# Encoder with mixture of experts on one Trainium2 core: the stage from output projection to first expert in hand order, first pair's tokens by one-hot products

## The chip, the cores and the metric

The kernel runs on one core of one Trainium2 chip. The metric is the device time of one execution in microseconds (us), the median of several runs. Three runs of the kernel before gave 1571.79, 1573.48 and 1576.59 us.

## The reference

Two layers on 512 tokens of width 1024, fp32. In each, a mixer makes a 512x1024 concatenation of heads, which is multiplied with `w_out`; then comes a LayerNorm, then a mixture of 32 experts in 4 groups of 8 (best group, best two experts in it), then a LayerNorm again. What the change touches is this piece, once per layer:

```
x = layer_norm(ALPHA * x + concat @ w_out, ln1_g, ln1_b)          # 512 x 1024
grp, exp = x @ w_grp + b_grp, x @ w_exp + b_exp                   # 4 and 32 logits of a token
g = argmax(grp); top2 = top_k(exp[g], 2)                          # two experts of a token
for e in experts:
    h = silu(x[tokens of e] @ w_gate[e]) * (x[tokens of e] @ w_up[e])
    ffn[tokens of e] += gate * (h @ w_down[e])
x = layer_norm(ALPHA * x + ffn, ln2_g, ln2_b)
```

The weights of the experts are 6.3 MB each, some 200 MB per layer, and are read once.

## The kernel before, in words

Tokens stand in four tiles of 128. Weights come through 16 slots of 1 MB that are shared (`slot`, `free`) and, in the expert stage, 7 or 8 more; `pump` issues the next load on SP's queue as soon as a slot is free, so the expert weights of a layer begin to arrive during the output projection, until all slots are full. A further load is issued only when the first expert has given slots back.

**The stage in question, `out_rest`** (from L452), is written as a string of steps (`PLAN`, L37), one for each layer, that are issued in that order; TensorE's and VectorE's final order is the scheduler's, except where `<` in front of a step says that it is to come after the last marked instruction. The steps: `b` and `o` are the output projection of one tile (each of two halves of the heads: 24 matmuls of 512 columns); `n` is a tile's residual sum (L506) and LayerNorm (`layer_norm`, L545), after which the tile is written to DRAM (`x1d`, L509); `t` turns a tile by eight transposes and two ScalarE copies (`moe_turn`); `l` makes its 36 logits by eight matmuls and adds the bias (`moe_logits`, L977, L981); `r` chooses the two experts and builds the one-hot slots (`moe_route`, L983); `H` and `R` give slots back; `S` is below. Tiles 1 and 2 are routed together, by instructions of twice the width. LayerNorm has a short form, two VectorE instructions (L558, L559) around GpSimd's power (L555, L556), and a long one on ScalarE, VectorE and GpSimd; the plan says which tile has which.

`moe_route` finds a maximum, marks where it stands, weighs the marks to keep the first, and does this for group, best and second expert. The marks of the two experts go to `rab` (L1028, bf16). TensorE counts by products with a triangle and with ones how many tokens before this one chose the same expert; with that `rpos` (L1035) holds a token's place and `S` (L1037) is, for four experts, a one-hot matrix of tokens by 64 places.

Step `S` (`start`) multiplies `S` with the token numbers (`moe_tokens`, `idr`), gets the row numbers `ridx` (L1095) and fetches the tokens of the pairs of experts 0 and 1 from `x1d` by an indirect DMA (`moe_fetch`, L1121). In `moe`, `moe_fit` (L1048) checks that no expert has more than 64 tokens; every engine loads that flag (`rover`) into a register and branches (L1283, L1284) past a general path, which is not taken with these inputs. Then `moe_gates` makes the gates, `features(0)` turns the fetched tokens by eight transposes into PSUM and a ScalarE copy (L1130), and the first expert's matmuls (`up`, 64x512 outputs) start. A pair of experts shares a 128-token tile.

Of the kernel before, what the change touches and what calls it, by code (L numbers as in the profile page):

```python
# [11 lines left out]
F32 = mybir.dt.float32  # L12
# [8 lines left out]
P = 128  # L21
D = 1024
# [14 lines left out]
PLAN = (("w w b2 b3 o0 H o2 n0 o1 o3 n2 R t0 n1 n3 <l0 <t3 <t1 <l1 <t2 l2 r0 <l3 r12 r3 S",  # L37
         (1, 3), (0, 2)),
        ("o0 o1 o3 o2 n1 R n0 <n3 n2 t3 <t1 <t0 <l1 t2 <l2 <l3 <l0 <r0 r12 r3 S",
         (1, 2, 3), ()))  # L40
# [41 lines left out]
class Kernel:  # L82
# [159 lines left out]
    def setup(self):  # L242
# [12 lines left out]
        wt = self.wt = c.tile([P, 8], F32, name="wt")  # L255
        for i in range(8):
            nc.gpsimd.memset(wt[:, i:i + 1], 0.5 ** i)
# [194 lines left out]
    def out_rest(self, pool, gbuf, m, plan, opt):  # L452


        res = [self.residual(m, t) for t in range(NT)]

        def begin(t):
            self.out_open(t)
            for q in self.order[:2]:
                self.out_mm(t, (2 * q, 2 * q + 1), q == self.order[0], False)  # L460

        def half_room():

            for q in self.order[:2]:
                self.free(*self.out_w[q])
            self.free(*self.catbuf.pop(self.order[0] // 2))

        def out(t):
            if t not in self.out_ps:
                begin(t)  # L470
            for q in self.order[2:]:
                if q not in self.out_w:
                    self.out_w[q] = self.next_w()
                self.out_mm(t, (2 * q, 2 * q + 1), False, q == self.order[-1])

        def turn(t):
            if t < 2:
                ps[t] = [self.pb()]
                halves = [ps[t][0][:, 0:512], ps[t][0][:, 512:D]]
                z = pool.tile([P, D], F32, name="mxT", bufs=2)  # L480
            else:
                halves = ps[t] = [self.pa(), self.pa()]
                z = rows[0][:, (t % 2) * D:(t % 2 + 1) * D]
            xT[t] = z.rearrange("p (j n) -> p j n", j=KJ)
            self.moe_turn(m, xT[t], res[t], halves)

        def logits(t):
            return self.moe_logits(m, xT[t], t, ps[t][0][:, 0:36])

        def route(*ts):  # L490

            z = ps[ts[-1]]
            last, f = self.moe_route(m, pool, ts, z[0][:, 512:D] if len(z) == 1 else z[1])
            for t in ts:
                self.rel(*ps[t])
            late.append(f)
            return last

        ps, xT, late = {}, {}, []

        def norm(t):
            tiles, halves = self.out_ps.pop(t)
            w = D // len(tiles)
            for i, z in enumerate(tiles):
                x = res[t][:, i * w:(i + 1) * w]
                self.nc.vector.scalar_tensor_tensor(x, x, ALPHA, z, op0=OP.mult, op1=OP.add)  # L506
            self.rel(*tiles)
            last = self.layer_norm(pool, res[t], gbuf, t in opt[0], t in opt[1])
            self.nc.scalar.dma_start(self.x1d[t * P:(t + 1) * P, :], res[t])  # L509
            return last  # L510

        def room():

            self.spare += 4
            if len(self.catbuf) == 2:
                half_room()
            for q in self.order[2:]:
                self.free(*self.out_w[q])
            self.free(*self.catbuf.popitem()[1])
            rows.append(self.slot())  # L520
            m.update(xbuf=self.slot(), xr=self.slot(), sc=self.slot(F32R))
            m["S"] = m["sc"][:, 0:D].rearrange("p (t e n) -> p t e n", t=NT, n=CAP)
            self.nc.gpsimd.memset(m["xr"], 0.0)
            self.spare -= 4

        def start():

            self.free(rows.pop())
            for p in range(2):
                ps = self.pa()  # L530
                self.moe_tokens(m, m["S"][:, :, 2 * p:2 * p + 2], self.idr, ps, p)
                self.rel(ps)
                self.moe_fetch(m, p, False)

        rows = []
        steps = dict(b=begin, H=half_room, w=self.prep_w, o=out, n=norm, t=turn, l=logits, r=route, R=room, S=start)
        last = None
        for step in plan.split():
            with self.tc.issue_after(last.ins) if step[0] == "<" else nullcontext():
                step = step.lstrip("<")  # L540
                last = steps[step[0]](*(int(t) for t in step[1:])) or last
        for f in late:
            f()

    def layer_norm(self, pool, x, gbuf, short, pool_beta):  # L545

        nc = self.nc
        gb = gbuf.rearrange("p (k n) -> p k n", k=2)
        st = pool.tile([P, 4], F32, name="lnas", bufs=4)
        mean, var, rs, nmr = (st[:, i:i + 1] for i in range(4))  # L550
# [4 lines left out]
        nc.gpsimd.tensor_scalar(rs, var, 1.0, LN_EPS, op0=OP.mult, op1=OP.add)  # L555
        nc.gpsimd.tensor_tensor(rs, rs, self.mhalf[:, 0:1], op=OP.pow)  # L556
        if short:
# [1348 lines left out]
```

## Time and profile before

| | |
|---|---|
| median of three runs | 1573.48 us |
| the profiled execution, by the same clock | 1578.68 us |
| its span in the trace | 1576.7 us |
| PE busy | 1493.6 us (95%) |
| DVE, ACT, POOL busy | 679.7, 444.0, 200.6 us |
| mean granted TensorE clock | 0.973 of full |
| read from HBM | 463 MB |

All times in the trace are us from the start of the span. PE is TensorE's matmul stream, PEld its weight loads, PEq its sequencer, DVE VectorE, ACT ScalarE, POOL GpSimd, SPq SyncE's DMA queue. A row of the timeline has start, duration, engine, line, operation, output<-inputs, sizes and how many instructions it merges, and in brackets the engine's idle time before it with what ended it. A plain fp32 matmul stands in the trace as two records, a transpose or an fp32r matmul as one: the eight logit matmuls of a tile are 16 records.

### The profile page before, as it was taken

What the parts mean: (1) busy time and instruction counts of PE and PEld (TensorE: products, weight loads), DVE (VectorE), ACT (ScalarE), POOL (GpSimd) and SP (SyncE); (2) the same over time, 40 slices, a digit from 0 to 9 for tenths busy, and PEclk for the clock granted to TensorE, in tenths of its full rate; (3) what the DMA queues carried; (4) which work ended last, traced back from release to release, by engine and by line L of the source; (5) the groups of instructions that cost most, each with busy time, mean ns of one, the idle gap of its engine ahead of it and who ended that gap; (6) DMA issues with size and microseconds to landing.
All of it is one profiled execution on the core that took longest, in us unless ns stands there. A gap on an engine that the chain in (4) does not pass through costs nothing. (4 is left out here: it accounts for less than half of the span.)

```text
span 1576.7 us, 19665 instructions
## 1 busy us (share of the span) xinstructions
PE 1493.6 (95%) x7801; PEld 897.0 (57%) x7801; DVE 679.7 (43%) x1198; ACT 444.0 (28%) x771; POOL 200.6 (13%) x296
## 2 busy tenths in 40 slices
PE   7999999879999999999999899996999999999997
PEld 6888888755444444444358687675444444444433
DVE  4555655443334334343445634364333433434334
ACT  4545522022121121111236534512212112111222
POOL 2322211321000000010022200031100000001001
PEclk9999999959999999999999999996999999999998
DMA  7311133759999999999963111276999999999993
GB/s 238 108 54 54 54 112 129 306 166 386 425 425 426 426 426 426 425 427 425 427 236 107 54 54 54 80 306 269 391 426 426 426 427 426 426 425 426 426 426 134
DMA packets 107131, 465.62 MB, mean 295 GB/s; under 512 B 13152, under 2 KB 48448, under 8 KB 57744
## 3 DMA queue, kind: packets, MB, share of 16 engines
q1 hardware_dynamic: 98848, 444.86, 69.5%
q0 software_dynamic: 6448, 13.06, 2.3%
q10 hardware_dynamic: 1728, 6.29, 1.1%
q8 instruction: 65, 1.06, 0.3%
q14 instruction: 42, 0.34, 0.1%
HBM read 463.16 MB, written 9.44 MB: 300 GB/s over the span
## 5 line engine op out<-in xcount | busy, mean ns | idle before, releaser
L217 PE MATMUL pa<-big 128*64 128x512 f32 (+3 forms) x4168 | 834.5, 460 | 10.3 <-ACT big L207 3.0
L217 PEld LDWEIGHTS pa<-big 128*128 128x128 f32 (+1 forms) x4168 | 451.6, 166 | 320.8 <-issue 273.9
L217 PE MATMUL pa<-big,hs 128*64 128x512 f32 x992 | 224.8, 592 | 0.0
L1187 DVE SCALAR_TENSOR_TENSOR big<-pa,rgate,big 64x512 fp32r<-64x512 f32 x120 | 90.0, 750 | 213.4 <-ACT big L1186 213.3
L1142 DVE SCALAR_TENSOR_TENSOR big<-big,pb 128x1024 f32<-128x1024 f32 x112 | 134.3, 1220 | 70.7 <-PE pb L217 68.8
L217 PEld LDWEIGHTS pa<-big,hs 128*64 128x64 f32 x992 | 72.9, 137 | 140.7 <-issue 136.2
L217 PE MATMUL pb<-big 128*128 128x512 f32 (+1 forms) x512 | 141.8, 414 | 5.2 <-DVE big L1142 4.2
L1186 ACT ACTIVATE big<-pa,rgate 64x512 fp32r<-64x512 f32 x120 | 81.9, 683 | 218.9 <-PE pa L217 170.2
L1157 DVE TENSOR_TENSOR h<-pa,h 64x512 f32<-64x512 f32 x64 | 44.4, 694 | 226.7 <-ACT h L1156 226.7
L217 PEld LDWEIGHTS pb<-big 128*128 128x128 f32 x512 | 91.3, 188 | 44.2 <-issue 20.2
L1156 ACT ACTIVATE h<-pa 64x512 f32<-64x512 f32 x64 | 37.7, 589 | 268.2 <-PE pa L217 268.2
L207 DVE TENSOR_TENSOR big<-big 128x2048 fp32r<-128x2048 f32 (+2 forms) x38 | 77.3, 2033 | 66.2 <-ACT big L207 47.4
L207 ACT CAST big<-big 128x2048 fp32r<-128x2048 f32 (+2 forms) x39 | 64.7, 1664 | 57.6 <-PE pa L217 22.5
L1121 POOL DMA_INDIRECT big<-x1d,ridx x32 | 34.0, 1062 | 356.1 <-DVE ridx L1095 269.2
L1120 POOL MEMSET big<- 128x1024 f32 x28 | 26.7, 955 | 315.8 <-PE pb L222 315.7
L1130 ACT COPY big<-pb 128x1024 f32<-128x1024 f32 x32 | 32.4, 1012 | 120.8 <-PE pb L222 120.8
L222 PE MATMUL pb<-eye,big 128*128 128x128 f32 x304 | 46.4, 298 | 20.0 <-DVE y L1082 6.2
L222 PEld LDWEIGHTS pa<-eye,h 64*128 64x128 f32 x256 | 35.5, 209 | 37.9 <-DVE big L1187 24.3
L217 PE MATMUL pb<-big,C 128*128 128x512 f32 x192 | 53.9, 412 | 2.5 <-DVE big L1142 2.5
L222 PEld LDWEIGHTS pb<-eye,big 128*128 128x128 f32 x304 | 40.7, 196 | 25.5 <-issue 20.1
L1167 DVE COPY hs<-pa 128x256 f32<-128x256 f32 x64 | 27.0, 422 | 43.6 <-PE pa L222 43.5
L217 PEld LDWEIGHTS pb<-big,C 128*128 128x128 f32 x192 | 33.3, 188 | 19.4 <-issue 9.7
(326 smaller groups left out, 1228.2 us busy)
## 6 DMA issues: line engine op xcount, KB each, us to landing
big<-in_moe_w_gate_dram SPq DMA_DIRECT2D x128, 1024.0 KB, 19.5
big<-in_moe_w_up_dram SPq DMA_DIRECT2D x128, 1024.0 KB, 19.6
big<-in_moe_w_down_dram SPq DMA_DIRECT2D x128, 1024.0 KB, 19.6
big<-in_ev_w_in_dram SPq DMA_DIRECT2D x24, 512.0 KB, 5.6
big<-in_od_w_in_dram SPq DMA_DIRECT2D x7, 1024.0 KB, 5.6
big<-in_x_dram SPq DMA_DIRECT2D x8, 512.0 KB, 4.2
big<-in_ev_w_out_dram SPq DMA_DIRECT2D x4, 1024.0 KB, 4.7
x1d<-big ACTq DMA_DIRECT2D x8, 512.0 KB, 7.8
```

What stands on the lines that cost most here:

```text
L207: ins = self.nc.scalar.copy(hi, src), (sub or self.nc.vector).tensor_tensor(lo, src, hi.bitcast(F32), op=OP.subtract)
L217: return self.nc.tensor.matmul(o, a, b, start=start, stop=stop, skip_group_check=True)
L222: self.nc.tensor.transpose(o, a, self.eye[s, s])
L1120: self.nc.gpsimd.memset(x, 0.0)
L1121: self.nc.gpsimd.indirect_dma_start(x, None, self.x1d[:, :], bass.IndirectOffsetOnAxis(m["idx"][:, pair:pair + 1], 0), bounds_check=T - 1, ...
L1130: self.nc.scalar.copy(xn, ps.rearrange("p (j n) -> p j n", j=KJ))
L1142: self.nc.vector.scalar_tensor_tensor(x, x, ALPHA if first else 1.0, ps, op0=OP.mult, op1=OP.add)
L1156: self.nc.scalar.activation(h, o[0:64], AF.Silu)
L1157: self.nc.vector.tensor_tensor(h, o[64:128], h, op=OP.mult)
L1167: self.nc.vector.tensor_copy(hs.rearrange("p j n -> p (j n)"), ps[:, 0:4 * CAP])
L1186: last = self.nc.scalar.activation(hi, src, AF.Copy, scale=g[a:a + 64])
L1187: self.nc.vector.scalar_tensor_tensor(yl[a:a + 64, s], src, g[a:a + 64], hi.bitcast(F32), op0=OP.mult, op1=OP.subtract)
```

## The change

- The two plan strings go. The steps of both layers stand as one list of calls inside a manual schedule that fixes the order on TensorE and VectorE. Tile by tile: the last output projections carry the turn and the logits of tiles 0 and 1 between them, and the choice of a tile's experts runs on VectorE between the norms.
- All tiles have the short LayerNorm, split into `ln_stats` and `ln_apply`; adding epsilon moves from GpSimd to VectorE.
- The choice (`moe_choose`) works on all 32 expert logits, with the other groups pushed down by -3e38, always on one tile, 13 instructions of VectorE. It writes `A0` and `A1`, which were made later before.
- The tokens of pair 0 are no longer fetched: `gather(t)` multiplies a tile's normalised tokens with its one-hot slots, eight fp32 matmuls of 128x128 per tile, summed over tiles in PSUM and copied by two ScalarE copies into `xbuf`. So `features(0)` and its fetch go. Pair 1 is fetched as before.
- Half of the projection's slots are given back before tile 0's projection in both layers (only in layer 0 before), and the working slot `rows` is not needed.
- `moe_fit` moves ahead of the last gather.

```diff
@@ out_rest @@
+        def half_room():
+            self.spare += 3
...
+            m.update(xbuf=self.slot(), xr=self.slot(), sc=self.slot(F32R))
...
+        def gather(t):
+            if t == 0:
+                m["g"] = self.pb()
+            xv = res[t].rearrange("p (k j) -> p j k", j=KJ)
+            S = m["S"][:, t, 0:2].bitcast(F32).rearrange("p e n -> p (e n)")
+            for j in range(KJ):
+                self.mm(m["g"][:, j * P:(j + 1) * P], xv[:, j, :], S, t == 0 and j % 4 == 0, t == NT - 1)
...
-        for step in plan.split():
-            with self.tc.issue_after(last.ins) if step[0] == "<" else nullcontext():
-                step = step.lstrip("<")
-                last = steps[step[0]](*(int(t) for t in step[1:])) or last
+        with self.tc.manual_schedule(engines={mybir.EngineType.PE, mybir.EngineType.DVE}):
+            begin(2)
+            begin(3)
+            half_room()
+            out(0)
+            norm(0, total(0))
+            out(1)
+            norm(1, total(1))
+            out(2)
+            turn(0)
+            norm(2, total(2))
+            out(3, last[0])
+            logits(0)
+            choose(0)
+            turn(1)
+            out(3, last[1])
+            room()
+            st = total(3)
+            logits(1)
+            count(0)
+            place(0)
+            norm(3, st)
+            turn(2)
+            choose(1)
+            logits(2)
+            count(1)
+            place(1)
+            gather(0)
+            choose(2)
+            turn(3)
+            gather(1)
+            count(2)
+            place(2)
+            logits(3)
+            gather(2)
+            choose(3)
+            count(3)
+            pc = self.moe_fit(m)
+            place(3)
+            gather(3)
+            self.moe_fits(m, pc)
+            for t in range(NT):
+                self.moe_slots(m, t, 1)
+            z = self.pa()
+            self.moe_tokens(m, m["S"][:, :, 2:4], self.idr, z, 1)
+            self.rel(z)
+            self.moe_fetch(m, 1, False)
+            for a in range(2):
+                s = slice(a * 512, (a + 1) * 512)
+                nc.scalar.copy(m["xbuf"][:, s], m["g"][:, s])
@@ ln_stats, ln_apply (layer_norm before) @@
-        nc.gpsimd.tensor_scalar(rs, var, 1.0, LN_EPS, op0=OP.mult, op1=OP.add)
-        nc.gpsimd.tensor_tensor(rs, rs, self.mhalf[:, 0:1], op=OP.pow)
+        nc.vector.tensor_scalar(st[:, 2:3], st[:, 1:2], LN_EPS, None, op0=OP.add)
+        nc.gpsimd.tensor_tensor(st[:, 2:3], st[:, 2:3], self.mhalf[:, 0:1], op=OP.pow)
...
+        self.nc.vector.scalar_tensor_tensor(x, x, st[:, 0:1], gb[:, 0], op0=OP.subtract, op1=OP.mult)
+        self.nc.vector.scalar_tensor_tensor(x, x, st[:, 2:3], gb[:, 1], op0=OP.mult, op1=OP.add)
@@ moe_choose (moe_route before) @@
+        def first_hot(o, v, mx, k, op):
+            fm = r.tile([P, 1], F32, name="fm", bufs=8)
             nc.vector.tensor_reduce(mx, v, axis=AX.X, op=OP.max)
+            nc.vector.scalar_tensor_tensor(o, v, mx, wt[:, 0:k], op0=OP.is_equal, op1=OP.mult, accum_out=fm)
+            nc.vector.tensor_scalar(o, o, 2.0, fm, op0=OP.mult, op1=op)
...
+        first_hot(A0, s, m["m12"][:, 0, t:t + 1], NE, OP.is_gt)
+        nc.vector.scalar_tensor_tensor(s, A0, -3.0e38, s, op0=OP.mult, op1=OP.add)
+        first_hot(A1, s, m["m12"][:, 1, t:t + 1], NE, OP.is_gt)
+        nc.vector.tensor_tensor(m["ab"][:, t, :], A0, A1, op=OP.add)
@@ moe @@
-        self.moe_fit(m)
...
-            features(0)
             up(0, 0)
```

TensorE in layer 0, from the last output projections to the first counts; before:

```order
L217 MATMUL pa<-big 128x512 x30
L217 MATMUL pb<-big 128x512 x24
L217 MATMUL pa<-big 128x512 x24
L217 MATMUL pb<-big 128x512 x24
L217 MATMUL pa<-big 128x512 x24
L222 MATMUL pb<-eye,big 128x128 x8
L222 MATMUL pa<-eye,big 128x128 x8
L222 MATMUL pb<-eye,big 128x128 x8
L217 MATMUL pa<-y_106,big 128x36 x4
L217 MATMUL pb<-y_106,mxT 128x36 x16
```

The same place in the change (its matmuls are issued at L213, its transposes at L218):

```order
L213 MATMUL pb<-big 128x512 x48
L213 MATMUL pa<-big 128x512 x24
L218 MATMUL pb<-eye,big 128x128 x8
L213 MATMUL pa<-big 128x512 x12
L213 MATMUL pb<-y_106,mxT 128x36 x8
L218 MATMUL pb<-eye,big 128x128 x8
L213 MATMUL pa<-big 128x512 x12
L213 MATMUL pb<-y_106,mxT 128x36 x8
L213 LDWEIGHTS tri
L213 MATMUL pb<-rab,tri 128x32
L218 MATMUL pa<-eye,big 128x128 x8
```

The turns (`eye`) and logits (128x36) of tiles 0 and 1 have moved in among the projections of tile 3, and the rest of the tiles follow one by one; the projections of 512 columns are as many as before.

VectorE in layer 0, from the last tile's sum (L506) to the first choice; before:

```order
L506 SCALAR_TENSOR_TENSOR big<-big,pa 128x512 x2
L553 BN_STATS lnst<-big 128x6 x2
L554 BN_AGGR lnas<-lnst 128x2
L558 SCALAR_TENSOR_TENSOR big<-big,lnas 128x1024
L559 SCALAR_TENSOR_TENSOR big<-big,lnas 128x1024
L981 TENSOR_TENSOR y_106<-pb,y_106 128x36 x2
```

In the change, from the end of tile 0's choice (`rab`) over the last tile's sum (L490) to the start of tile 1's choice:

```order
L1042 TENSOR_TENSOR rab<-y_106 128x32
L490 SCALAR_TENSOR_TENSOR big<-big,pa 128x512 x2
L592 BN_STATS lnst<-big 128x6 x2
L593 BN_AGGR lnas<-lnst 128x2
L594 TENSOR_SCALAR lnas<-lnas 128x1
L1053 SCALAR_TENSOR_TENSOR rpos<-pb,rab 128x32
L1057 TENSOR_TENSOR big<-io,rpos 128x128
L600 SCALAR_TENSOR_TENSOR big<-big,lnas 128x1024
L601 SCALAR_TENSOR_TENSOR big<-big,lnas 128x1024
L1021 TENSOR_TENSOR y_106<-pb,y_106 128x36
```

Tile 3's sum and norm now stand behind the choice of tile 0, and the choice of tile 1 behind that norm.

TensorE in layer 0, end of the stage; before:

```order
L217 LDWEIGHTS tri
L217 MATMUL pa<-rab,tri 128x32
L217 LDWEIGHTS ones
L217 MATMUL pa<-rab,ones 128x32
L217 MATMUL pa<-idr,big 128x2 x2
L1283 TENSOR_LOAD rover
L1284 COMPARE_AND_BRANCH
```

and in the change:

```order
L213 LDWEIGHTS ones
L213 MATMUL pa<-rab,ones 128x32
L213 MATMUL pb<-big 128x128 x8
L213 MATMUL pa<-idr,big 128x2 x4
L1300 TENSOR_LOAD rover
L1301 COMPARE_AND_BRANCH
```

The last gather (`pb<-big 128x128 x8`) has come in between the counts and the load of the flag; behind the branch, the eight transposes of the fetched tokens are gone, so that the first expert follows.

## Rows read from the trace of the kernel before

**Rows 1.** The page, part 2: what the DMA engines moved in 40 equal slices.
```profile
GB/s 238 108 54 54 54 112 129 306 166 386 425 425 426 426 426 426 425 427 425 427 236 107 54 54 54 80 306 269 391 426 426 426 427 426 426 425 426 426 426 134
```

**Rows 2.** Timeline of PE at the end of either expert stage.
```profile
787.03 3.65 PE L217 MATMUL pa<-big 128*64 128x512 f32 x14 [1.43 <-DMA big<-in_moe_w_up_dram]
...
1534.16 3.65 PE L217 MATMUL pa<-big 128*64 128x512 f32 x14 [1.35 <-DMA big<-in_moe_w_up_dram]
```

**Rows 3.** Windows of 1 us on PE, layer 0: busy (instructions), granted clock, DMA share, GB/s.
```profile
317.00:318.00 1.00, 1.00 (x7) 0.50 1.07 287
...
320.00:321.00 1.00, 1.00 (x11) 1.00 0.98 397
...
324.00:325.00 1.00, 1.00 (x7) 0.50 1.06 446
...
330.00:331.00 1.00, 1.00 (x7) 0.50 0.00 0
...
354.00:355.00 1.00, 1.00 (x8) 1.00 0.00 0
```

**Rows 4.** Timeline of PE, layer 0, output projection to first expert.
```profile
290.02 5.60 PE L217 MATMUL pb<-big 128*128 128x512 f32 x24
...
306.34 5.61 PE L217 MATMUL pa<-big 128*128 128x512 f32 x24
...
317.47 1.91 PE L222 MATMUL pb<-eye,big 128*128 128x128 f32 x8
...
344.43 1.94 PE L222 MATMUL pb<-eye,big 128*128 128x128 f32 x8 [6.24 <-DVE y L1082]
347.47 13.53 PE L217 MATMUL pa<-big 128*64 128x512 f32 x48 [1.10 <-ACT big L1130]
```

**Rows 5.** Timeline of PE, layer 1, the same stage.
```profile
1045.80 16.48 PE L217 MATMUL pa<-big 128*128 128x512 f32 x72
...
1096.30 12.88 PE L217 MATMUL pa<-big 128*64 128x512 f32 x48 [1.54 <-ACT big L1130]
```

**Rows 6.** Matmuls of 16 or 32 records: 36 and 128 columns; eight transposes (PE).
```profile
1067.74 1.95 PE L217 MATMUL pb<-y,mxT 128*128 128x36 f32 x16
...
327.93 3.63 PE L217 MATMUL pa<-y,big 128*128 128x36 f32 x16
...
1109.10 1.15 PE L222 MATMUL pb<-eye,big 128*128 128x128 f32 x8
...
273.32 3.74 PE L217 MATMUL pa<-rvg,pt 128*128 128x128 f32 x32
```

**Rows 7.** Timeline of DVE, layer 0: a short norm, tile 3's last choice, its slots.
```profile
308.88 1.22 DVE L506 SCALAR_TENSOR_TENSOR big<-big,pb 128x1024 f32<-128x1024 f32 x1
...
313.70 1.28 DVE L559 SCALAR_TENSOR_TENSOR big<-big,lnas 128x1024 f32<-128x1024 f32 x1 [0.72 <-POOL lnas L556]
...
335.42 0.16 DVE L998 TENSOR_REDUCE y<-sel 128x1 f32<-128x8 f32 x1
...
336.16 0.17 DVE L1026 TENSOR_TENSOR o<-o,o 128x8 f32<-128x8 f32 x1
...
337.12 0.42 DVE L1037 TENSOR_TENSOR big<-io,rpos 128x256 fp32r<-128x256 f32 x1
```

**Rows 8.** Timeline of POOL, layer 0: epsilon of the norm in rows 7.
```profile
311.75 1.28 POOL L555 TENSOR_SCALAR lnas<-lnas 128x1 f32<-128x1 f32 x1 [0.38 <-DVE lnas L554]
```

**Rows 9.** Timeline of DVE, layer 1: tile 3's slots, the last to be made.
```profile
1087.37 0.43 DVE L1037 TENSOR_TENSOR big<-io,rpos 128x256 fp32r<-128x256 f32 x1
```

**Rows 10.** PE's sequencer at the branch (both layers), and at an earlier flag's load.
```profile
L1284 PEldq COMPARE_BRANCH  x2: 3326/4546/5765, 338.2 to 1088.3; - x2
...
L1619 PEldq TENSOR_LOAD <-steep x1: 314/314/314, 1012.5 to 1012.5; - x1
...
1014.30 3.89 PE L217 MATMUL pb<-big 128*128 128x512 f32 x14
```

**Rows 11.** The chain that ended last: up matmuls of later experts.
```profile
1142.75 10.45 PE pa L217 x48
```

More of the change, by code (lines that the diff above doesn't have):

```diff
@@ L254, in setup @@
         nc.vector.memset(self.ones, 1.0)
-        wt = self.wt = c.tile([P, 8], F32, name="wt")
-        for i in range(8):
-            nc.gpsimd.memset(wt[:, i:i + 1], 0.5 ** i)
+        wt = self.wt = c.tile([P, NG, EPG], F32, name="wt")
+        for i in range(EPG):
+            nc.gpsimd.memset(wt[:, :, i], 0.5 ** i)
         tid = self.tid = c.tile([P, NT], F32, name="tid")
@@ L490, in route @@
[L490 to L537, printed above, removed]
-        for step in plan.split():
-            with self.tc.issue_after(last.ins) if step[0] == "<" else nullcontext():
-                step = step.lstrip("<")
-                last = steps[step[0]](*(int(t) for t in step[1:])) or last
@@ L542, in out_rest, with choose, count, place @@
-        for f in late:
-            f()
-    def layer_norm(self, pool, x, gbuf, short, pool_beta):
+            z = ps[t]
+            self.moe_logits(m, xT[t], z[0][:, 0:36])
+            ps[t] = z, z[0][:, 0:36], (z[0][:, 512:D] if len(z) == 1 else z[1])[:, 0:NE]
+        def choose(t):
+            self.moe_choose(m, pool, t, ps[t][1])
+        def count(t):
+            self.moe_count(m, t, ps[t][2])
+        def place(t):
+            self.moe_place(m, t, ps[t][2], 0)
+            self.rel(*ps[t][0])
@@ L547, in layer_norm, with ln_stats @@
+    def ln_stats(self, pool, x):
         nc = self.nc
-        gb = gbuf.rearrange("p (k n) -> p k n", k=2)
-        st = pool.tile([P, 4], F32, name="lnas", bufs=4)
-        mean, var, rs, nmr = (st[:, i:i + 1] for i in range(4))
+        st = pool.tile([P, 3], F32, name="lnas", bufs=4)
         bs = pool.tile([P, 2, 6], F32, name="lnst", bufs=2)
@@ new lines, in moe_count, with moe_place, moe_slots @@
+    def moe_count(self, m, t, o):
+        ab = m["ab"]
+        for u in range(t):
+            self.mm(o, self.ones, ab[:, u, :], u == 0, False)
+        self.mm(o, self.tri, ab[:, t, :], t == 0, True)
+    def moe_place(self, m, t, o, pair):
+        self.nc.vector.scalar_tensor_tensor(m["pos"][:, t, :], o, 1.0, m["ab"][:, t, :], op0=OP.add, op1=OP.mult)
+        self.moe_slots(m, t, pair)
+    def moe_slots(self, m, t, pair):
+        self.nc.vector.tensor_tensor(m["S"][:, t, pair % 2 * 2:pair % 2 * 2 + 2], self.io[:, None, :].to_broadcast([P, 2, CAP]),
+                                     m["pos"][:, t, 2 * pair:2 * pair + 2, None].to_broadcast([P, 2, CAP]), op=OP.is_equal)
@@ L1051, in moe_fit, with moe_fits @@
             self.mm(pc[:, 0:NE], self.ones, m["ab"][:, t, :], t == 0, t == NT - 1)
+        return pc
+    def moe_fits(self, m, pc):
+        nc = self.nc
         nc.vector.tensor_reduce(m["keep"], pc[:, 0:NE], axis=AX.X, op=OP.max)
```

126 lines of the change are left out of this document (48 added, 78 removed).

## The prediction

> **What bounds the kernel now.** I read the slices of the page first. In two long stretches, one for each expert stage, the DMA engines move 425 to 427 GB/s, slice after slice [rows 1]: the expert weights come as fast as they ever do. The timeline of TensorE at the end of both stages then shows it waiting for a weight, by 1.43 and 1.35 us only [rows 2]. So weight stream and TensorE run out together, and the stream cannot be ahead: shortly before and after the first expert starts nothing moves, as at 330 and 354 in layer 0 [rows 3], since all slots are full. What counts is therefore when the first expert starts in each layer; its matmuls give the first slots back, and stream and TensorE shift with it, one to one. The change touches nothing behind that point but the work that it drops.
>
> In layer 0 the last projection ends at 306.34 + 5.61 = 311.95 us and the first expert starts at 347.47 [rows 4]; in layer 1 at 1045.80 + 16.48 = 1062.28 and 1096.30 [rows 5]. That is 35.5 and 34.0 us in which TensorE mostly waits for VectorE, for the branch and for the fetched tokens. I follow the changed stage through layer 0 and carry it to layer 1 by the distance of the projections' ends, 750.33 us.
>
> **The change, part by part.** *TensorE up to the last projection.* The projection of tile 2 ends, as tile 1's or 2's did before, 3 x 5.44 us after 290.02, at 306.3 [rows 4]. Then come, at full clock: turn(0) 1.0, half a projection 2.7, logits(0) 2.0, turn(1) 1.0, half a projection 2.7 [rows 4, 6]. The last projection ends at 315.7, 3.8 us later than before; the time is not lost, the same turns and logits came after it.
>
> *VectorE.* This is the longest chain. A short norm takes 313.70 + 1.28 - 308.88 = 6.1 us, 0.72 of it a stall [rows 7]: GpSimd's little instruction stood for 1.28 us beside a VectorE instruction of 128x1024 [rows 8], where the power came after it. Moving epsilon to VectorE (0.15 us more there) leaves the power; I let it stand behind the same instruction as epsilon did, so the stall stays. If not, 0.7 us is won on each of three tiles, 2 us per layer. The first three norms: 295.7 + 3 x 6.25 = 314.4. A choice: maximum, marks and threshold take 336.16 - 335.42 = 0.74 us [rows 7], slightly more on 32 columns, three times 2.3; four more instructions at 0.23 with their gaps 0.9; together 3.2 us. So choose(0) ends at 317.6, tile 3's sum and statistics (3.0: the 6.1 less stall and two multiplications of 1.28, with epsilon) at 320.6, place(0) at 321.2 (0.2 and, for 128 columns by the 256 that took 0.42, some 0.3), two multiplications at 323.8, choose(1) at 327.1, and with a count (0.3 for a few narrow records, an estimate by [rows 6]) and place(1) before it choose(2) at 331.1.
>
> *The gathers.* They are 4 x 8 new matmuls per layer. At full clock 32 records of 128 columns took 3.74 us [rows 6], so 16 take 1.9. At half clock none is in the trace: eight transposes of 128 columns took 1.94 [rows 4] and 16 logit records 3.63 [rows 6], which bounds 16 records between 3.6 and 3.9; I take 3.8. The clock thus decides what 7.5 to 15 us of gathers, two turns and two or three sets of logits cost.
>
> *The clock.* It is granted in two levels. In layer 0 it was half at 317; transposes of 128 columns ran without a gap until 319.4 [rows 4], and at 320 it was full; then came mostly logits of 36 columns, and at 324 it was half, as it still was at 330, though TensorE was busy without a pause [rows 3, 6]. [...] In the change logits(1), turn(2), logits(2) and a wait until 327.1 lose it; then gather(0), turn(3) and gather(1) stand without a gap. I take half clock for the first two (3.8 + 1.9, until 332.9) and full from there: gather(1) 334.9, count(2) 335.1, logits(3) 337.1, choose(3) behind it 340.4; count and place(3) give the last one-hot slots at **341.2**. Before, they were done at 337.12 + 0.42 = 337.54 [rows 7]. So routing ends 3.7 us later: four narrow choices instead of three, one of them double, with norms and gathers between them. The same steps with 1.9, 1.0 and 2.0 for gather, turn and logits (full clock) give 338.2, with 3.8, 1.9 and 3.6 (half) 344.7.
>
> *From the slots to the first expert.* Before: 347.47 - 337.54 = 9.9 us in layer 0 and 1096.30 - 1087.80 = 8.5 in layer 1 [rows 4, 5, 7, 9]: token numbers, load of the flag, the branch, which held TensorE's sequencer for 5.77 and 3.33 us [rows 10], the longer in layer 0 (6.24 us of idle [rows 4]), then eight transposes (1.94) and a ScalarE copy with its handovers (1.1 [rows 4]). In the change transposes and copy are gone; gather(3) and the copies run beside the branch, if the sequencer reaches it before the array has finished. It does so elsewhere: a flag was loaded at 1012.5 while matmuls that stand ahead of it in the program started at 1014.30 [rows 10]. The flag is ready some 0.6 us after the slots (three small instructions of about 0.17 [rows 7]); with 0.3 for its load, 3.3 for the branch and 0.1 that is 4.3 us. Gather(3) at 1.9 to 3.8 and 1.5 for the copies, two in place of one, are 3.4 to 5.3. I take 5.0, and 0.7 more in layer 0, whose branch was the longer; why it was is not shown, and the other end, 2.5, is kept for the range. The fetch of pair 1 starts later, but features(1) needs it 13 us after the first expert has begun, and token numbers, fetch and all took 9.9 before: nothing. The gates come after the branch as before: nothing. Dropping the late `A0`, `A1`: nothing, VectorE waits there.
>
> Layer 0: 341.2 + 5.7 = 346.9, against 347.47: -0.6. Layer 1: 341.2 + 5.0 + 750.3 = 1096.5, against 1096.30: +0.2.
>
> *The first expert's clock.* Its first 48 records took 13.53 and 12.88 us, against 10.45 at full clock [rows 4, 5, 11]. With the last gather shortly before, part of these 3.1 and 2.4 us may go; I take 1.0 of 5.5.
>
> The sum is -0.6 + 0.2 - 1.0 = -1.4 us. The profiled execution took 1578.68 us (span 1576.7) and would take 1577.3; it lies 5.2 above the median of the three runs, 1573.5, so I forecast a median of **1572.0 us**, no change: a measurement of this kernel can tell about 0.3%, 4.7 us, from none.
>
> **The rivals.** *A: the clock holds (faster).* If gathers and turns keep it at full, or win it back at once, slots are done at 338.2; with 4.3 for the path (0.7 more in layer 0) the first experts start at 343.2 and 1092.8, -4.3 and -3.5, and with up to 5.5 for a first expert at full clock that is -8 to -13 us: about 1563. A power that does not stall (2 us per layer) leads the same way. For it: wide matmuls did bring the clock back [rows 3]. Against: VectorE's choices leave TensorE waiting 4 us and more between the tiles.
>
> *B: half clock all the way (slower).* Slots at 344.7, and behind them gather(3) and copies, 5.3: 350.7 in layer 0 and 1100.3 in layer 1, +3.2 and +4.0, and 2 more if the branch in layer 0 stays at 5.8: +7 to +9, about 1581. The point that decides is whether the stretch of gather(0), turn(3), gather(1) brings the clock back. For it: in layer 0 the clock was half at 324 and at 330 beside a fully busy TensorE [rows 3]. The Trainium skill (TensorE: Matmul & The Clock Gate, Part 4: PE-mode transpose) says that transposes do not bring the full clock; the transposes until 319.4 here, with full clock at 320, speak against it [rows 3, 4]. By that rule turn(3) would not count, and the time would be B's.
>
> *C: the sequencer does not run ahead.* Then load and branch stand behind gather(3) and the token numbers: 7.4 us instead of 5.0, +2.4 in each layer, total +3.4, about 1577; with a low clock it falls to B's side. Against it: [rows 10].
>
> *D: the change does not reach the end.* If the weight stream had slack, an earlier start would be swallowed. The waits [rows 2] leave 1.4 us for that; it speaks for no change either way.
>
> **How the numbers follow.** The forecast has 0.42, A 0.32, B 0.18, C 0.08, half of it beyond the bound. D changes nothing. Faster by over 0.3%: 0.32. Within: 0.42 + 0.04 = 0.46. Slower: 0.18 + 0.04 = 0.22. The range takes A's middle and B's upper value, 1562 to 1582; beyond it lie the full 13 us of A and a B with C.
>
> **What would show it.** Right: the first expert (48 records, 64-wide) starts within 2 us of 347 and 1097; the last one-hot slots lie 3 to 4 us later than before; the path from there is 3 to 5 us shorter; VectorE is busy from 296 to 331 without long gaps; the clock is half when gather(0) begins and full before gather(2). Wrong: gathers of 3.8 us everywhere (B), of 1.9 everywhere (A), a flag loaded only after the last gather's end (C), a branch far from 3.3 us, a power that overlaps VectorE's multiplication, or an end of the run that does not move with the first experts.

## The result, and the profile after

| | before | change |
|---|---|---|
| median of four runs on the same chip | 1574.47 us | 1595.39 us (1594.33 to 1596.72) |
| ratio, 95% interval | | 1.0134 (1.0116 to 1.0153) |
| profiled execution, its span | 1578.68, 1576.7 us | 1594.33, 1592.2 us |

The change is 21 us slower; 1572.0 and "no change" were forecast. The first place to look is the one that the forecast took as given, the rate of the weights. The page's part 2, what the DMA engines moved in 40 slices; of the change:

```profile
GB/s 236 107 54 54 54 133 106 298 164 398 421 419 419 421 421 419 420 420 421 419 246 94 54 75 32 123 338 186 396 420 420 419 421 421 419 419 420 421 420 137
```

Every full slice is at 419 to 421 where it was at 425 to 427 [rows 1]. 402 MB of expert weights take 13.5 us more at 420.3 than at 426.3 GB/s.

The timeline of PE in layer 0, against [rows 4]:

```profile
271.99 3.74 PE L213 MATMUL pa<-rvg,pt 128*128 128x128 f32 x32
...
304.99 0.60 PE L218 MATMUL pb<-eye,big 128*128 128x128 f32 x4
307.20 0.71 PE L218 MATMUL pb<-eye,big 128*128 128x128 f32 x4 [1.61 <-ACT mxT L1010]
...
313.54 0.71 PE L218 MATMUL pb<-eye,big 128*128 128x128 f32 x4 [0.68 <-ACT mxT L1010]
314.01 2.98 PE L213 MATMUL pa<-big 128*128 128x512 f32 x12
...
318.56 1.13 PE L218 MATMUL pa<-eye,big 128*128 128x128 f32 x8
...
325.53 4.17 PE L213 MATMUL pb<-big 128*128 128x128 f32 x16
329.49 1.91 PE L218 MATMUL pa<-eye,big 128*128 128x128 f32 x8
331.20 3.90 PE L213 MATMUL pb<-big 128*128 128x128 f32 x16
...
335.01 1.95 PE L213 MATMUL pa<-y,mxT 128*128 128x36 f32 x16
336.80 4.15 PE L213 MATMUL pb<-big 128*128 128x128 f32 x16
...
341.75 4.11 PE L213 MATMUL pb<-big 128*128 128x128 f32 x16 [0.59 <-DVE big L1057]
...
350.15 13.30 PE L213 MATMUL pa<-big 128*64 128x512 f32 x48 [3.95 <-DVEq L1301]
```

The rows of 16 records `pb<-big 128x128` are the gathers, 3.9 to 4.2 us each. Windows inside gather(0) and gather(1), with their length, PE busy, granted clock (1.00 is full), DMA share and GB/s:

```profile
325.50:329.40 3.90, 3.89 (x17) 0.50 1.01 418
331.20:335.00 3.80, 3.80 (x20) 0.94 0.39 164
```

So the first ran at half clock, the second almost all at full, and they took 4.17 and 3.90 us. The last row of the timeline is the first expert.

VectorE in the same place, against [rows 7]: the place of tile 2, the last slots, the flag, the token numbers, the first work behind the branch.

```profile
335.29 0.19 DVE L1053 SCALAR_TENSOR_TENSOR rpos<-pa,rab 128x32 f32<-128x32 f32 x1 [5.94 <-PE pa L213]
...
341.40 0.29 DVE L1057 TENSOR_TENSOR big<-io,rpos 128x128 fp32r<-128x128 f32 x1
...
341.83 0.15 DVE L1072 TENSOR_SCALAR rover<-rkeep 128x1 int32<-128x1 f32 x1
...
346.24 0.16 DVE L1113 TENSOR_SCALAR ridx<-pa 128x1 int32<-128x1 f32 x1 [3.26 <-PE pa L213]
350.10 0.18 DVE L1080 TENSOR_TENSOR y<-y 128x16 f32<-128x16 f32 x1 [3.71 <-DVEq L1301]
```

The flag is written at 341.83, but each engine loads it (L1300) and branches (L1301) in its own order; instructions of these lines in both layers, shortest, median and longest duration in ns, first and last start:

```profile
L1300 PEldq TENSOR_LOAD <-rover x2: 307/399/491, 343.0 to 1102.1; - x2
L1300 ACTq TENSOR_LOAD <-rover x2: 278/375/472, 345.9 to 1105.1; - x2
L1300 DVEq TENSOR_LOAD <-rover x2: 304/426/548, 346.3 to 1105.7; - x2
...
L1301 PEldq COMPARE_BRANCH  x2: 3528/3654/3781, 343.6 to 1102.6; - x2
...
L1301 DVEq COMPARE_BRANCH  x2: 56/64/72, 346.9 to 1106.1; - x2
L1301 DVEq EVENT_SEMAPHORE  x2: 21/21/21, 349.9 to 1106.7; - x2
```

TensorE's sequencer does run ahead: load at 343.0, while gather(3) runs until 345.9. ScalarE and VectorE don't: their loads, at 345.9 and 346.3, stand behind the copies and the token numbers, which stand behind gather(3). VectorE comes out at 349.9, and the first expert starts at 350.15. From its branch instruction to the next of its sequencer VectorE took 3.0 us in layer 0 (346.9 to 349.9) and 0.6 in layer 1 (1106.1 to 1106.7).

Layer 1, from an anchor ahead of the stage:

```profile
1009.60 7.13 PE L213 MATMUL pa<-big 128*128 128x512 f32 x16
...
1089.46 1.04 PE L218 MATMUL pa<-eye,big 128*128 128x128 f32 x8
1090.35 3.97 PE L213 MATMUL pb<-big 128*128 128x128 f32 x16
...
1107.18 11.96 PE L213 MATMUL pa<-big 128*64 128x512 f32 x48 [1.49 <-DVE y L1083]
```

Here the turn takes 1.04, full clock, and the gather behind it 3.97 all the same.

**Milestones.** Runs reach the stage some 3 us apart in layer 0 and 11 in layer 1, so times below count from a matmul ahead of it that all of them have: in layer 0 the 32 records `rvg,pt` (271.99 in the change, 273.32 before), in layer 1 the 16 of 7.13 us (1009.60, 1003.65). "Second profile" is run g1 below, the kernel before with its slots elsewhere.

| us from the anchor | before [rows 4, 5, 7, 9] | second profile | forecast | change | aligned change (f1) |
|---|---|---|---|---|---|
| layer 0: last projection ends | 38.6 | 38.6 | 42.4 | 45.0 | 45.1 |
| layer 0: last one-hot slots | 64.2 | 64.4 | 67.9 | 69.7 | 69.8 |
| layer 0: first expert | 74.2 | 74.2 | 73.6 | 78.2 | 78.3 |
| layer 1: last projection ends | 58.6 | 58.6 | - | 67.4 | 65.9 |
| layer 1: last one-hot slots | 84.2 | 80.6 | 87.9 | 91.2 | 89.8 |
| layer 1: first expert | 92.7 | 88.9 | 92.9 | 97.6 | 96.0 |

Anchor and first expert of layer 1, in g1 and then in f1:

```profile
1002.70 7.13 PE L217 MATMUL pa<-big 128*128 128x512 f32 x16
...
1091.62 12.89 PE L217 MATMUL pa<-big 128*64 128x512 f32 x48 [1.10 <-ACT big L1130]
```

```profile
1005.47 7.13 PE L213 MATMUL pa<-big 128*128 128x512 f32 x16
...
1101.51 13.49 PE L213 MATMUL pa<-big 128*64 128x512 f32 x48 [1.38 <-DVE y L1080]
```

Of the change's 67.4 for layer 1's last projection, 1.5 us against f1's 65.9 are one half projection that ran at half clock, 4.56 us against 3.02.

### The profile page after: what moved, and what is told of

Read it like the earlier page. It is cut to its first block, busy times and chain, and to the rows that moved or that the text cites. A ratio compares the mean times of both kernels' runs of the same rounds, so it can differ in the third digit from the quotient of the medians.

```text
span 1592.2 us, 19865 instructions
## 1 busy us (share of the span) xinstructions
PE 1513.1 (95%) x7905; PEld 915.1 (57%) x7905; DVE 692.0 (43%) x1215; ACT 440.2 (28%) x770; POOL 188.0 (12%) x278
## 3 DMA queue, kind: packets, MB, share of 16 engines
q1 hardware_dynamic: 98848, 444.86, 69.8%
## 5 line engine op out<-in xcount | busy, mean ns | idle before, releaser
L213 PE MATMUL pa<-big 128*64 128x512 f32 (+3 forms) x4168 | 838.6, 461 | 18.1 <-DMA big<-in_moe_w_up_dram 7.2
L213 PEld LDWEIGHTS pa<-big 128*128 128x128 f32 (+1 forms) x4168 | 453.0, 166 | 329.9 <-issue 278.5
L213 PE MATMUL pa<-big,hs 128*64 128x512 f32 x992 | 224.9, 592 | 0.0
L213 PE MATMUL pb<-big 128*128 128x512 f32 (+2 forms) x640 | 173.9, 418 | 6.3 <-DVE big L1160 4.1
L213 PEld LDWEIGHTS pa<-big,hs 128*64 128x64 f32 x992 | 72.6, 137 | 141.0 <-issue 136.1
L213 PEld LDWEIGHTS pb<-big 128*128 128x128 f32 x640 | 122.7, 217 | 51.0 <-issue 26.0
L218 PEld LDWEIGHTS pa<-eye,h 64*128 64x128 f32 x256 | 35.4, 209 | 37.8 <-DVE big L1205 23.5
L213 PE MATMUL pb<-big,C 128*128 128x512 f32 x192 | 53.9, 412 | 2.5 <-DVE big L1160 2.5
L218 PE MATMUL pb<-eye,big 128*128 128x128 f32 x288 | 42.6, 288 | 12.4 <-DMA big<-in_x_dram 5.9
L218 PEld LDWEIGHTS pb<-eye,big 128*128 128x128 f32 x288 | 37.3, 195 | 18.5 <-issue 7.5
L213 PEld LDWEIGHTS pb<-big,C 128*128 128x128 f32 x192 | 33.3, 188 | 19.4 <-issue 9.7
```

Source lines behind the costliest of these rows:

```text
L213: return self.nc.tensor.matmul(o, a, b, start=start, stop=stop, skip_group_check=True)
L218: self.nc.tensor.transpose(o, a, self.eye[s, s])
```

## The experiments

**The slower weights: where the slots lie.** The change widens a constant in `setup`, `wt`, from 8 to 32 columns. It is allocated ahead of the weight slots, so all of them move up by 96 bytes of a partition: the first from byte 23296 to 23392. Small constants behind `wt` move too, but of what moves only the slots are filled by the stream of weights. Run e1 makes only this step in the kernel before; e2, f1 and f2 pad the change so that its slots begin at 23424, 23552 and 23808; g1 moves those of the kernel before to 23552.

```diff
-        wt = self.wt = c.tile([P, 8], F32, name="wt")
+        wt = self.wt = c.tile([P, 32], F32, name="wt")                        # e1
+        wt = self.wt = c.tile([P, NG + 1, EPG], F32, name="wt")[:, 0:NG]      # e2; f1 + 5, f2 + 13
```

e1: 

> The kernel before with its table of powers widened from 8 to 32 columns (only 8 used), so that all weight slots lie 96 bytes higher in SBUF, as in the change; nothing else differs. Theory S (the weight stream is slower because of where its slots lie): full slices at 419 to 421 GB/s instead of 425 to 427; 402 MB at 420.3 instead of 426.3 take 13.5 us more, so 1587 to 1589 us. Rival P (the stage that was rewritten slows the stream, by what it leaves in the queues or slots): 426 GB/s and 1574 us, as before. Rival R (the stream's rate differs from build to build with no rule): anything, but no repeat of 420.

e2: 

> The change with its table widened by 8 more columns (32 bytes), so that the slots lie on a multiple of 64 bytes as before. Theory S: full slices back at 425 to 427 GB/s and 13.5 us less than the change's 1595.4, so 1580 to 1584 us; what is left over the kernel before (some 8 us) is the stage's own. Rival P: 420 GB/s and 1595 us.

f1: 

> The change with 160 bytes of padding: slots begin at byte 23552 of a partition (46 x 512). Before: 23296 (91 x 256; 426 GB/s); shifted or changed so far: 23392 and 23424 (no multiple of 256; 420 GB/s). Theory S256 (slots at multiples of 256 bytes stream faster): 425 to 427 GB/s and 13.5 us less than the change, 1580 to 1584 us. Theory S512 (it is an offset of 256 in 512 that is good): 420 and 1595. Rival R (no rule of addresses, each build has a rate of its own): cannot be told by one, but this one and f2 would not agree with either rule.

f2: 

> The change with 416 bytes of padding: slots begin at 23808 (93 x 256, the same place within 512 bytes as the kernel before's 23296). S256 and S512 both: 425 to 427 GB/s, 1580 to 1584 us. If this one is at 420 and 1595 too, the address is not what counts, or only in larger units.

g1: 

> The kernel before with its slots moved from byte 23296 to 23552, both multiples of 256. Theory S256: no change, 425 to 427 GB/s and 1570 to 1575 us. It is also a second profile of the kernel before: in the first one TensorE's clock was half for 8 us of layer 1's stage (logits 3.42 and 3.63 us where the shifted kernel's profile has 1.95 and 1.98). If that is chance, this one reaches layer 1's first expert some 3 us sooner, counted from the 16 matmuls of 7.13 us that stand ahead of the stage in either: 89 us instead of 92.65. Rival S512 (512 streams faster still): above 427 GB/s and under 1568.

| run | first slot at | GB/s of full slices | median us | ratio to before (95%) |
|---|---|---|---|---|
| the change | 23392 | 419 to 421 | 1595.39 | 1.0134 (1.0116 to 1.0153) |
| e1, before | 23392 | 419 to 421 | 1587.07 | 1.0105 (1.0079 to 1.0131) |
| e2, change | 23424 = 183 x 128 | 419 to 421 | 1596.39 | 1.0169 (1.0146 to 1.0191) |
| f1, change | 23552 = 92 x 256 | 425 to 427 | 1584.31 | 1.0069 (1.0046 to 1.0091) |
| f2, change | 23808 = 93 x 256 | 425 to 427 | 1582.98 | 1.0066 (1.0046 to 1.0086) |
| g1, before | 23552 | 425 to 427 | 1572.20 | 0.9999 (0.9979 to 1.0019) |

A ratio is against the kernel before, run beside it on the same chip, so ratios compare better than medians. The same row of the page, e1 first, then f1:

```profile
GB/s 236 108 54 54 54 109 131 308 174 382 420 420 420 420 420 420 420 420 419 421 244 112 64 54 54 76 310 294 403 420 420 420 420 421 420 419 420 420 421 128
```

```profile
GB/s 237 107 54 54 54 123 117 273 188 369 426 425 426 426 427 425 426 426 426 426 251 95 54 58 51 103 336 206 376 426 426 427 426 426 426 426 426 426 426 133
```

The 96 bytes alone slow the kernel before by 12 to 21 us, and slots at a multiple of 256 take 11 to 12 off the change by the medians (1595.39 against 1584.31 and 1582.98), 10 to 11 by the ratios (1.0134 against 1.0069 and 1.0066); the rate alone would make 13.5. e2, with the same rate as the change, came out 0.35%, 5 us, above it by its ratio, so these sizes are good to some 5 us. A multiple of 128 (e2) is not enough, where I had guessed 64; three starts at multiples of 256 are fast, whether or not they are multiples of 512, two others are slow. The Trainium skill (DMA: Bandwidth & Descriptors, How a descriptor splits into AXI transactions) says that a transfer is cut into pieces of at most 256 bytes, each of which must start at a multiple of 256, so that one which starts elsewhere also fetches the bytes ahead of its start; it speaks of reads, while here the slots are the side that is written. What the pieces do inside no run shows.

g1 also answers a doubt on the first profile of before. Logits of layer 1's stage, first profile, then g1:

```profile
1069.97 3.42 PE L217 MATMUL pb<-y,mxT 128*128 128x36 f32 x16
...
1074.97 3.63 PE L217 MATMUL pa<-y,big 128*128 128x36 f32 x16
```

```profile
1069.02 1.95 PE L217 MATMUL pb<-y,mxT 128*128 128x36 f32 x16
...
1072.15 1.98 PE L217 MATMUL pa<-y,big 128*128 128x36 f32 x16 [0.23 <-ACT big L975]
```

The same work ran at half clock in one execution and at full in the other, and with it layer 1's first expert came at 92.7 or 88.9 us. My base for layer 1 was an execution in which it was 3.7 late.

**What the gathers cost.** With the rate restored, f1 is left 0.7%, 11 us, behind the kernel before. f3 takes the gathers out and puts fetch and `features(0)` back. e5 and e4 give them weights that lie side by side, by a ScalarE copy of each tile, in fp32 and in fp32r (which makes one record of a matmul instead of two); their slots lie as in e2, so e2 (1596.39) is their base. f4 is e4 on f1's slots, with the copies behind those of the turns and the slots freed behind the branch.

```diff
-            gather(0)                                                          # f3: all four
+            nc.scalar.copy(own(t), res[t].rearrange("p (k j) -> p j k", j=KJ))  # e4, e5, f4
-            xv = res[t].rearrange("p (k j) -> p j k", j=KJ)
-            S = m["S"][:, t, 0:2].bitcast(F32).rearrange("p e n -> p (e n)")
+            xv = own(t)
+            S = m["S"][:, t, 0:2].rearrange("p e n -> p (e n)")                # e5 keeps the bitcast
```

e5: 

> As e4, but the copy stays fp32 and the products too, so that against e2 only the stride of the weights is gone (and ScalarE has four copies more). Theory G: a gather's 16 records take 1.9 us at full clock and 3.8 at half, against 4.1 at either in e2; slots and first expert 4 to 5 us earlier in each layer: e2 minus 8 to 10 us. Rival W (it isn't the stride, fp32 records with 128 columns of new weights each take 0.25 us): gathers of 4 us, e2 within 2 us.

e4: 

> e2 with the gathers made cheap: ScalarE copies each normalised tile, rounded to fp32r and with a feature chunk's columns side by side, and the eight matmuls of a gather take these contiguous weights in fp32r, one record each instead of two. Theory G (a gather takes 4.1 us because of its strided fp32 weights, and count(2) on TensorE waits behind two gathers while VectorE idles 5.9 us): a gather takes 1.0 us at full clock and up to 2 at half, VectorE's wait before the place of tile 2 nearly goes, the last slots lie 6 to 7 us earlier than in e2, the first expert too, in each layer: e2 minus 12 to 14 us, 1568 to 1571. Rival H (the gathers only fill waits of VectorE's chain or of the branch): e2 within 3 us.

f3: 

> f1 with one part of the change undone: the tokens of pair 0 are fetched by the indirect DMA and turned after the branch, as before, and the gathers are gone; the hand order and the choice tile by tile stay. Theory G (the gathers in front of count(2), count(3) and of the tokens of pair 1 hold VectorE's chain): in layer 0 the last slots at some 335.0 us instead of 341.7, first expert 335.0 + 9.9 = 345 instead of 350; layer 1 by as much; total f1 minus 8 to 12 us. Rival V (VectorE's longer chain of choices is what costs, the gathers lie beside it): f1 plus 0 to 6 us, since transposes and fetch come back.

f4: 

> f1 with the cheap gathers of the fp32r run, mended in two places: ScalarE's four copies stand behind the turns' copies instead of ahead of them (there they held the projection of tile 3 for 3.5 us), and the two slots that hold them are given back behind the branch (there a weight load was issued just before it, and SyncE and VectorE came out of it 5.5 to 6.3 us after entering, against 2.5 to 3.1 in the change). Theory: gathers of 1.1 to 1.95 us, last slots at some 336.5 in layer 0, branch as in the change, first expert at 343 to 345 instead of 350 and some 7 us earlier in layer 1: f1 minus 10 to 14 us, 1568 to 1573. Rival B (the branch costs what it costs, weights in flight or not, and grows when all engines reach it at once): first expert 349, f1 minus 0 to 4.

Gathers in e5's timeline, at half and at full clock:

```profile
327.78 3.76 PE L213 MATMUL pb<-big 128*128 128x128 f32 x16
...
332.90 1.95 PE L213 MATMUL pb<-big 128*128 128x128 f32 x16
```

The weight loads of the four gathers of layer 0, grouped by shape, in the change and then in e5 (busy us, mean ns):

```profile
L213 PEld LDWEIGHTS pb<-big 128*128 128x128 f32 x64 | 15.6, 335 | 3.6 <-issue 2.9 <-DVE big L1057 0.7
```

```profile
L213 PEld LDWEIGHTS pb<-big 128*128 128x128 f32 x64 | 9.1, 226 | 3.6 <-issue 2.9 <-DVE big L1063 0.7
```

So it is the stride. The gather's weights are `x` with every eighth column, 32 bytes apart; side by side they cost what the forecast had assumed, 3.8 and 1.9. The Trainium skill (SBUF — State Buffer, Specifications) says that reads which land in a new 16-byte line each time are slower; 32 bytes do that, and the trace agrees, 335 against 226 ns a load, means over stretches at both clocks.

Times fell short of what these runs were to bring. e5 (1600.29) and e4 (1594.97) gained nothing on e2: ScalarE's copies, 2.0 to 2.2 us each, stood ahead of the turns' copies, so that the last projection ended at 48.5 (1.5 us of it a half projection at half clock) and 46.9 us instead of 45.0; and a weight load issued at the branch left TensorE idle for 6.8 and 7.2 us before layer 0's first expert, 3.95 in the change. f3, without gathers, took 1581.65 (ratio 1.0059, 1.0037 to 1.0080): slots 4.6 us earlier than f1 in layer 0, 4.0 in layer 1, first expert 3.0 and 1.6, and transposes and copy back in the path; that is 2.7 us less than f1 where 8 to 12 were expected. f4 took 1575.29 (1.0018, 1.0006 to 1.0030), 9 less than f1 (8 by the ratios): first expert at 73.5 and 93.7 instead of 78.3 and 96.0, gathers of 1.95 us, but at half clock throughout:

```profile
327.62 1.95 PE L213 MATMUL pb<-big 128*128 128x128 f32 x8
...
332.85 3.61 PE L213 MATMUL pa<-y,mxT 128*128 128x36 f32 x16
```

The logits that had 1.95 behind the change's long gathers take 3.61 behind the short ones here; in e4, behind gathers as short, they had 1.95, so no rule follows. f4 changes stride, number format and copies together: that the stride alone makes a gather long is shown by e5, what it alone costs the whole kernel is not.

**The order.** In the cuts from here on calls are put on one line and shortened. g2 gives layer 1 its old order of projections, on f1; g3 puts tile 3's turn and logits ahead of the gathers, on f4; g4 has both.

```diff
-            begin(2); begin(3); half_room(); out(0)       # g2, layer 1
+            out(0)                                        # begin(2) ahead of out(2), begin(3) ahead of out(3)
-            logits(2); count(1); place(1); gather(0); choose(2); turn(3); gather(1); count(2)      # g3
+            logits(2); turn(3); count(1); place(1); logits(3); gather(0); choose(2); count(2)
```

g2: 

> f1 (the change, aligned) with the order of layer 1's projections as it was before: tiles 0 and 1 are finished first, and the first halves of tiles 2 and 3 stand behind them instead of ahead. In the change they stand ahead in both layers, and VectorE's first sum of layer 1 comes 42.9 us behind the 16 matmuls of 7.13 us, against 37.4 in the shifted kernel before. Theory L (this later start is a cost of its own in layer 1): first sum at 37.4 again, first expert 3 to 6 us earlier in layer 1, f1 minus 3 to 6 us: 1578 to 1581. Rival T (TensorE ends the last projection at the same time either way, and what follows it is what counts): first expert within 1 us of f1's, 1583 to 1585.

g3: 

> f4 with tile 3's turn and logits ahead of the first gather and the gathers behind the counts that VectorE waits for. In f4 VectorE idles 1.7 us before the place of tile 2 and 2.9 before the choice of tile 3 (layer 0). Theory: both waits go, last slots 4 to 4.5 us earlier in each layer, first expert too: f4 minus 7 to 9 us, 1566 to 1568. Rival B (the branch and the restart of the engines behind it set the first expert): f4 within 3 us.

g4: 

> g3 with the order of layer 1's projections of g2. Theory: the two add up, 1561 to 1565 us, below both kernels. Rival M (with the first expert of layer 1 as early as this the weights have not filled their slots by then, since the slots of the projection are given back later, and the stream sets the end): as g3 within 2 us.

g2 was slower, 1586.49, by 2.2 us against f1 by the medians and 4.4 by the ratios: nothing was left for TensorE to do while weights were split. Two of its waits ahead of the first projection:

```profile
1028.84 0.80 PE L218 MATMUL pa<-eye,on 128*128 128x128 f32 x4 [2.63 <-DVE on L975]
...
1035.51 12.77 PE L213 MATMUL pb<-big 128*128 128x512 f32 x47 [1.53 <-DVE big L203]
```

Its waits come to 6.6 us there, f1's to 2.5, and the 47 records behind them took 12.77 us where f1's 48 took 11.04. VectorE's first sum came 3.9 us sooner, the last projection at 71.9 instead of 65.9, and the first expert at 102.6 instead of 96.0; g4 (1581.21, 1.0048) ends 6.4 us behind g3, with its first expert of layer 1 at 99.0 instead of 92.7. g3 itself, 1574.79 (1.0010, 0.9996 to 1.0024), was the puzzle: last slots 2.9 and 3.1 us earlier than f4's, first expert 0.3 and 1.0.

**The branch.** In g3 a weight load was issued between SyncE's flag load and its branch. h1 ties the loads of the two copies' slots to an instruction behind the branch; h2 adds another order for layer 1.

```diff
-        self.free(*m.pop("xg"))                          # h1
         self.moe_gates(m)
+        for x in m["xg"]:
+            nc.vector.tensor_tensor(m["Z0"][:, 0, 0:1], m["Z1"][:, 0, 0:1], x[:, 0:1].bitcast(F32), op=OP.mult)
+        self.free(*m.pop("xg"))
...
+            begin(2); out(0); norm(0, total(0)); out(1); norm(1, total(1)); begin(3)     # h2, layer 1
```

h1: 

> g3 with the weight loads of the two slots that hold the copies tied to an instruction behind the branch. In g3 one of them was issued between SyncE's load of the flag and its branch (337.18 in layer 0); 242 and 381 GB/s moved while the engines went through the branch, TensorE's took 5.9 and 7.0 us (3.4 to 3.8 in f1 to f4, with almost nothing moving) and SyncE came out 6.5 us behind it. So the last slots were 4.7 us earlier than f4's, counted from the same event, and the first expert 0.3. Theory Q (what crosses the branch waits behind weight transfers): TensorE's branch 3.4 to 3.8 us, first expert 3 us earlier in each layer than g3's, g3 minus 4 to 7 us: 1568 to 1571. Rival E (all engines reach the branch within 2 us of each other here, and that is what makes it long): 5.9 to 7 us again, 1573 to 1576.

h2: 

> h1 with another order in layer 1: first half of tile 2, tiles 0 and 1 to their end, then the first half of tile 3, and turn, logits and choice of tile 0 ahead of the end of tile 2. In g2 the plain old order made TensorE wait 6.6 us for weights that were still being split; here the half of tile 2 stands in that place. Theory L: VectorE's first sum of layer 1 at 37.4 us behind the matmuls of 7.13 instead of 42.7, its chain ends some 4 us earlier, h1 minus 3 to 5 us. Rival M (slots of the projection come free 11 us later in layer 1, so weights still move when the branch comes, and it costs the 3 us that h1 won there, or the stream sets the end): h1 minus 1 to plus 3.

(The 4.7 us of the expectation for h1 are counted from the start of the span; from the anchor the slots of g3 lie 2.9 us before f4's.) TensorE's branch, then windows of 2 us (PE busy, granted clock, DMA share, GB/s); g3 first, then h1:

```profile
L1314 PEldq COMPARE_BRANCH  x2: 5876/6422/6968, 337.9 to 1085.7; - x2
```

```profile
340.00:342.00 2.00, 0.00 (x0) 0.50 1.09 381
...
1088.00:1090.00 2.00, 0.00 (x0) 0.50 0.88 295
```

```profile
L1314 PEldq COMPARE_BRANCH  x2: 3296/3362/3428, 339.1 to 1087.8; - x2
```

```profile
340.00:342.00 2.00, 0.00 (x0) 0.50 0.07 25
...
1088.00:1090.00 2.00, 0.84 (x5) 0.50 0.03 8
```

Theory Q holds here: with weights moving the branch takes 5.9 to 7.0 us, without 3.3 to 3.4, though in h1 too the engines reach it within 2 us of each other. How far it goes is open: h2's layer 0 took 4.3 us with 16 and 109 GB/s beside it and no load issued, and g1's two branches took 5.2 and 4.3 us, with 385 and 221 and with 107 and 142 GB/s. The long branch of layer 0 before [rows 10] fits it, though no run undid that one; the same columns beside the two branches of the kernel before (ahead of the clock, the busy time of PE, PEld, DVE, ACT and POOL):

```profile
338.00:340.00 2.00, 0.19 (x1) 0.10 (x1) 0.59 (x4) 1.28 (x1) 1.23 (x2) 0.50 0.81 315
...
1088.00:1090.00 2.00, 0.44 (x2) 0.35 (x2) 0.37 (x3) 1.24 (x1) 1.15 (x1) 0.50 0.08 20
```

The kernel before does issue further loads ahead of the first expert, which its description and the prediction did not count on: SyncE issued weight loads at 331.63 and some 336.6 us in layer 0, and the first expert starts at 347.47.

From the last slots to the first expert h1 took 6.9 and 5.9 us, g3 9.5 and 8.5. The first expert came only 1.1 and 2.6 us sooner than in g3, since in layer 0 the last half projection ran at half clock (4.58 us against 3.03) and the slots came 1.5 later. The time is 1573.85 (0.9993, 0.9980 to 1.0005), 0.9 less than g3 by the medians and 2.7 by the ratios, where 4 to 7 were expected: from the first expert to the end of layer 0's expert stage it took 2.1 us longer, with two slots filled later. h2 took 1573.61 (0.9999, 0.9986 to 1.0013). Its first sum in layer 1 came at 37.2 instead of 42.7, but the last projection at 65.5 and the first expert at 90.3, in h1 at 90.1: TensorE's total up to the last tile counts there, not VectorE's start, so theory L fell.

## Why the prediction was wrong

- **"The change touches nothing behind that point but the work that it drops", and so a stream at 425 to 427 GB/s.** This step cost the most, 10 to 12 of the 21 us: the slots moved by 96 bytes, and the stream ran at 419 to 421 GB/s. Without it the change (f1, 1584.31) would still lie beyond the range. The diff of `setup` showed the wider `wt`; I read it as a constant and not as something that moves all that is allocated behind it.
- **"The last projection ends at 315.7."** 42.4 us from the anchor, measured 45.0. I let a turn's eight transposes run in one go; the second four wait for ScalarE's copy of the first, 1.61 us in turn(0), whose copy also stands behind the issue of two DMAs, and 0.68 in turn(1). In these two turns both halves are written into one tile (`pb`); turns 2 and 3, which write into two (`pa`), do run their eight in one go, 1.13 us in turn(2).
- **VectorE** was right: choose(2) was to end at 331.1, 57.8 us from the anchor, and did at 57.4.
- **"16 take 1.9", 3.8 at half clock.** The size was off, not the mechanism: 3.9 to 4.2 at either. The rows that I priced it by [rows 6] had weights side by side. That puts the last slots 1.8 us later than forecast, and gather(3) on the path.
- **"I take 5.0, and 0.7 more in layer 0"** from slots to first expert: 8.5 and 6.4. I followed TensorE's sequencer, which did what I said (rival C, which put the wait there, is out), and not the flag's load on ScalarE and VectorE, which stands behind gather(3) on these engines; VectorE's branch adds 3.0 us in layer 0 and 0.6 in layer 1.
- **Layer 1 carried over by 750.3 us.** Its tail was shorter: 22.0 us from last projection to last slots (80.6 - 58.6) in the undisturbed profile, 25.8 in layer 0 (64.4 - 38.6). The change has 23.9 and 24.7 (f1), so a projection that ends 7.3 and 6.5 us later costs more in layer 1: first expert +7.1 against +4.0. And the row I compared with, 1096.30 [rows 5], was itself late by a clock at half, which hid 3.7 us of that.
- **First expert's clock, -1.0.** Layer 0's expert stage and the mixer behind it took 1.5 us less in f1 than in g1, and the last stretch 1.5 more: nothing.

f1 against g1: 4.0 - 1.5 + 7.1 + 1.5 = 11.1 us; the ratio of 1.0069 says 10.8. With the 10 to 12 of the slots that makes 21 to 23 of the 20.9 us measured. Rival B named the right sign, but for half clock; in layer 0 the clock was half through gather(0) and turn(3) and full in gather(1), as forecast, then half again in gather(3), and in layer 1 turn(3) already had full clock. No run shows what brings the clock back. Shown by an experiment of its own are the slots, the stride and the branch; the turns' waits are read from the trace, and no run undid them alone.

None of the versions beats the kernel before: f4, g3, h1 and h2 come back to it within 0.2% (1.0018, 1.0010, 0.9993, 0.9999).

## What to carry to other kernels

A tile that grows moves every tile that is allocated behind it: after a change that "only" widens a constant, compare the start addresses of the buffers that a DMA-bound stream fills, and the GB/s of its full slices. Price a matmul by a row whose weights have the same stride, not only the same shape. On a path through a branch, follow the flag on every engine that has to take it, and look at what moves on the DMA engines meanwhile.

## What the runs showed of the hardware

- Transfers into slots that begin at a multiple of 256 bytes of a partition ran at 425 to 427 GB/s, at 23392 and 23424 at 419 to 421, with as many packets.
- fp32 weights read 32 bytes apart made 16 records of 128 columns take 3.9 to 4.2 us at either clock, against 1.95 and 3.76 side by side.
- A branch past code that isn't run took TensorE 3.3 to 4.3 us with no weight load issued beside it (h1, h2, the change), and 5.9 to 7.0 with 240 to 380 GB/s (g3).
- The same instructions of layer 1's stage were granted half clock in one execution of the kernel before and full clock in another.
